# A one-core transformer layer: seven edits to where work stands in the order

## The chip, the core and the metric

The kernel runs on one core of one Trainium2 chip. A core has five engines, each with its own in-order instruction queue: PE (TensorE, the matrix engine; its weight loads are shown apart as PEld), DVE (VectorE), ACT (ScalarE), POOL (GpSimd) and SP (SyncE, which here only issues DMA transfers). They meet through semaphores. The metric is the device time of one execution in microseconds (us), and smaller is better.

## The reference, cut to what matters

One step of a streaming encoder layer. The two inputs are a prompt of 1024 frames and 64 frames of a running stream (1088 tokens in all), with a model width of 1024.

```python
mod = silu(c) @ w_ada + b_ada                                # shift1, scale1, gate1, shift2, scale2, gate2
h = rms_norm(x, g_norm1) * (1 + scale1) + shift1
c_q, c_kv, k_rope_raw, gq, gk, gv, g_lr, g_r = split(h @ w_in)
# group A: latent attention, 4 heads, chunk mask of 64 frames
latent = concat([past_latent, rms_norm(c_kv, g_kv_lora)])
kv = latent @ w_ukv                                          # per head: 128 key columns, 128 value columns
q = rms_norm(rms_norm(c_q) @ w_uq); k = rms_norm(concat([k_nope, krope]))   # then rotary, softmax, @ v
# group B: gated linear attention, 4 heads
log_a = log_sigmoid(g_lr @ w_gate_up + b_gate_up) / 16
b_out = rms_norm(gla_recurrence(gq, gk, gv, log_a, s0)) * silu(g_r)
x = x + gate1 * (concat([a_out, b_out]) @ w_out)
h2 = rms_norm(x, g_norm2) * (1 + scale2) + shift2
y = x + gate2 * (square(relu(h2 @ w_up)) @ w_down)           # MLP width 4096
```

The new latents, rotary keys and recurrent states are outputs too.

## The kernel before

All matrix products of the projections run three matmuls per block of 128 rows: operands are split into a rounded high part and the rest (`split`: an ACT copy makes the high part, a DVE subtraction the low part), and `mm3` (lines 93 to 95) multiplies high by high, high by low and low by high. So each operand costs an ACT and a DVE instruction before PE may use it, and most of PE's rows carry the lines 93, 94 and 95.

Tokens are in nine tiles (`TILES`: eight of 128 and one of 64, index 8, the running stream) or, for the first projections, three chunks (`CHUNKS`: 384, 384 and 320 tokens). PSUM has eight banks: four named `mm`, two named `tp` (transposes) and two named `g`.

What sets the order: each phase is a set of Python generators that yield (estimated PE time, wait, condition). `interleave` runs them against a made-up clock, always taking the first one that is ready, and the framework's own scheduler then places the instructions of each engine by its cost estimates, except those that `keep_in_program_order` pins. So a yield's number moves the place of what follows it only indirectly, and an edit in one generator moves others.

The stages that the change touches, in order of time:

- **First chunk** (`start`, `scales`, `normed`). While x, w_ada and the first columns of w_in are loaded, the sum of squares of chunk 0 is made: ACT squares eight blocks (line 325), DVE adds them 4+4, 2+2, 1+1 (line 330), PE sums over partitions (line 338), and the factor is spread by `dg` and a matmul with ones (line 357). PE makes the scale vector from w_ada (`scale_rows`, line 420), `scale_end` copies and transposes it (`lat`, lines 427 to 443). `split_first(hf, j)` makes `wh` and `wl` of half hf of column group j (lines 307 and 308). `normed` multiplies (line 378) and splits each block of x into `hh` and `hl`. Then `qk` runs group A0, A1 on the halves.
- **Gated linear attention** (`gla`). For each tile six or seven levels of `QL`,`KL` products (line 747), the output `o`, its norm `og` (line 802), and a `tail` that transposes og (line 808), scales it into `mog` and stores it. The tail of a tile runs within the next tile, at level 3.
- **Latents and gates** (`latents`, `gates`). `latents` runs the projection D1 (24 matmuls of 320 columns per tile), norms the 256 latent columns into `cn`, and one tile later transposes cn (line 644), scales it into `cl` (line 647, one buffer) and stores it in `lat_d`. At the same time `gates` takes, for each tile, g_r and the stored output of group B into two of four `gv` buffers (lines 825 and 826, both issued by SP), applies silu on ACT (line 829) and the product on DVE (line 830), and stores it (line 831).
- **Keys** (`keys_values`). Four tiles of past keys, then nine of new ones: 12 matmuls `g<-lath`, a norm over ACT, POOL and DVE (`kn`, line 907), then four transposes of kn (line 914) and four of the rotary part `krt` (line 921). The transposes stand behind a yield of 4500.
- **First MLP blocks** (`up`, `norm2`). The MLP runs a two-level product scheme with seven products per block. Product 1 of a block uses a `tp` bank. At the same time the last quarter of the second norm is under way: it spreads its factor into a `tp` bank (line 1387) that DVE reads in 16 instructions (line 1393).
- **Output** (`out`). The last product (4) of the down projection adds to 128 by 544 rows of y in two halves; the row block is stored once, after the second half.

Of the kernel before, what the change touches and what calls it, by code (L numbers as in the profile page):

```python
# [10 lines left out]
F32 = mybir.dt.float32  # L11
# [3 lines left out]
ALU = mybir.AluOpType  # L15
# [4 lines left out]
P = 128  # L20
# [11 lines left out]
HT = TOK // 2  # L32
# [39 lines left out]
def layer(ctx: ExitStack, tc: tile.TileContext, I, O):  # L72
# [12 lines left out]
    def tp_bank():  # L85
        return psT.tile([P, 512], F32, name="tp")
# [10 lines left out]
    def heads(ap):  # L97
        return ap.rearrange("p (h t) -> p h t", h=H)
# [176 lines left out]
    with ExitStack() as sctx:  # L275
# [43 lines left out]

        def scales(c):  # L320

# [6 lines left out]
            yield 600, 1000, None  # L328
            for n in (4, 2, 1):
                mm = DVE.tensor_tensor(out=sq[:, 0:n, :cn], in0=sq[:, 0:n, :cn],  # L330
                                                                   in1=sq[:, n:2 * n, :cn], op=ALU.add)
                if c == 0:
                    tc.keep_in_program_order(mm)
            yield 300, 1500 if c == 0 else 3000, None
            blocks = [(o, min(P, cn - o)) for o in range(0, cn, P)]
            pm = tp_bank()
            for j, (o, n) in enumerate(blocks):
                mm = PE.matmul(pm[:n, j:j + 1], lhsT=sq[:, 0, o:o + n], rhs=ones[:, 0:1], start=True, stop=True)
                if c == 0:
                    tc.keep_in_program_order(mm)  # L340
            st = xp.tile([P, 3], F32, name="st", bufs=2)
# [14 lines left out]
            for j, (o, n) in enumerate(blocks):  # L356
                mm = PE.matmul(bcs[c][:, o:o + n], lhsT=ones[:n, :], rhs=dg[:n, j, :n], start=True, stop=True)
                if c == 0:
                    tc.keep_in_program_order(mm)
            yield 600, 0, None  # L360

# [24 lines left out]
        def start():  # L386
            load_x(0)
            load_mod(0)
            load_first(0)
            load_mod(1)  # L390
            load_first(1)
            yield 0, 100, None
            load_x(1)
            acc = g_bank()
            for j in range(2):
                groups[GROUPS[j][0]] = [wp.tile([P, 8, 256], F32R, name=n) for n in ("wh", "wl")]
            a = scales(0)
            next(a)
            next(a)
            scale_rows(0, acc, range(4))  # L400
            next(a)
            scale_rows(0, acc, range(4, KT))
            for _ in a:
                pass
            split_first(0, 0)
            split_first(0, 1)
            scale_end(0, acc)
            yield 0, 0, has("mod 1 0")
            for n in "hl":
                h[n] = hpool.tile([P, KT, TOK + 2], F32R, name="h" + n)  # L410
            for c in range(3):
                if c:
                    yield 0, 4500, None
                    yield from scales(c)
                yield from normed(c)

# [118 lines left out]
    with gctx:  # L535
# [84 lines left out]
        def latents():  # L620
            yield 2000, 0, has("D1")
            for i in (8, 0, 1, 2, 3, 4, 5, 6, 7):
                off, n = TILES[i]
                s = i == 8
                ps = yield from rows("D1", off, n, 320)
                cn_ = dp.tile([P, 256], F32, name="cn")
                s2 = dp.tile([P, 2], F32, name="s2")
# [12 lines left out]
                while len(tails) > (0 if i == 7 else 1):  # L640
                    j, o2, n2, c2 = tails.pop(0)
                    tp = tp_bank()
                    for b in range(2):
                        PE.transpose(tp[:, b * P:b * P + n2], c2[:n2, b * P:(b + 1) * P], ident[:n2, :n2])
                    cl = dp.tile([P, 2, P], F32, name="cl", bufs=1)
                    for b in range(2):
# [8 lines left out]
        def gla():  # L655
# [56 lines left out]
            for i, (off, n) in enumerate(TILES):  # L712
# [23 lines left out]
                for lv, hf in enumerate(halves):  # L736
# [27 lines left out]
                    if lv == 2:  # L764
# [14 lines left out]
                        if i >= 7:  # L779
                            dst = O["st_s"] if smp else O["st_p"]  # L780
                            for p in range(2):
                                for j in range(2):
                                    SP.dma_start(dst[2 * p + j], sb_new[64 * j:64 * j + 64, p, P * j:P * j + P])
                    if lv == 3 and tail is not None:
                        tail()
                        tail = None
# [33 lines left out]
        def gates():  # L820

            yield 0, 2000, has("end C1", "gla out")
            for i, (off, n) in enumerate(TILES):
                r, mx = (gw.tile([P, 512], F32, name="gv", bufs=4) for _ in range(2))
                SP.dma_start(heads(r)[:, :, :n], r_d[:, :, off:off + n])
                SP.dma_start(heads(mx)[:, :, :n], mix_d[:, 4:8, off:off + n])
                yield 0, 1000, None
                r, mx = (heads(t)[:, :, :n] for t in (r, mx))
                ACT.activation(r, r, AF.Silu)
                (DVE if i % 2 else DVE).tensor_tensor(out=r, in0=r, in1=mx, op=ALU.mult)  # L830
                SP.dma_start(mix_d[:, 4:8, off:off + n], r)
# [44 lines left out]
    def keys_values(lh, ll, ki, tab, n, kv, slot):  # L876
# [33 lines left out]
        cs = slice(P * slot, P * slot + n)  # L910
        yield 0, 4500, None
        tp = heads(tp_bank())
# [506 lines left out]
    with ExitStack() as uctx:  # L1419
# [142 lines left out]
        def up():  # L1562
# [3 lines left out]
            def product(j, i, h):  # L1566
# [5 lines left out]
                elif i == 5:  # L1572
                    side[j, h] = g_bank()[:, 0:HT // 2]
                b = tp_bank()[:, 0:HT // 2] if i == 1 else side[j, h] if i > 4 else chain[j, h]
                for k in range(4):
# [101 lines left out]
    with ExitStack() as dctx:  # L1677
# [120 lines left out]
        def out(i, m, h, b):  # L1798
# [4 lines left out]
            for s, c0, c1 in SPANS:  # L1803
                c0, c1 = max(c0, h * HW), min(c1, h * HW + HW)
                if c0 < c1:
                    DVE.scalar_tensor_tensor(out=e[:, c0:c1], in0=b[:, c0 - h * HW:c1 - h * HW],  # L1806
                                             scalar=modT[:, 5, m0 + m, s:s + 1], in1=e[:, c0:c1], op0=ALU.mult, op1=ALU.add)
            if h and end:
                SP.dma_start(O["y_T"][(m0 + m) * P:(m0 + m + 1) * P, HT * th:HT * th + HT], e)

# [63 lines left out]
```

## Time and profile before

| | us |
|---|---|
| median of 3 runs | 1394.36 (1393.22 to 1397.86) |
| the profiled execution | 1394.88 |
| its span, first to last instruction | 1393.1 |
| PE busy in it | 1340.9 (96%) |
| PEld, DVE, ACT busy | 1261.0, 900.3, 685.3 |

A row of the timeline reads: start, duration, engine, line, operation, out<-in, partitions and elements, a count, and in brackets how long the engine sat idle before it and what it waited for. A row with a count stands for several instructions merged, and its duration is that of the group. Matmuls are pipelined: the step from one start to the next, not the duration, is what one costs. A row of the windows view reads: the stretch, its length, the busy time of each engine with its count of instructions, then the granted clock of PE as a share of full speed, the share of the DMA engines, and GB/s. A row of the waits view reads: who, for whom, total us, number of times, longest. A row of DMA issues gives the count, the size of each and the median time from issue to landing.

### The profile page before, as it was taken

The numbers are of one execution on the slowest core, as the hardware profiler recorded it, in microseconds if no ns is written. First come the engines' busy times: TensorE is split into PE (matmuls) and PEld (weight loads), VectorE is DVE, ScalarE is ACT, GpSimd is POOL, SyncE is SP. The second block draws the span as 40 slices with busy tenths as digits, with TensorE's granted clock in tenths as the row PEclk, the third lists the DMA queues.
The fourth block names the chain that finished last, engine by engine and source line by source line (L and its number), as shares of the span: only waits on it lengthen the run. The fifth ranks groups of instructions, "written<-read, shape, count | busy, mean of one in ns | idle before, by whom it ended". The sixth has DMA issues, their size and how long they took to land.

```text
span 1393.1 us, 26171 instructions
## 1 busy us (share of the span) xinstructions
PE 1340.9 (96%) x10014; PEld 1261.0 (91%) x10014; DVE 900.3 (65%) x2040; ACT 685.3 (49%) x1756; POOL 63.6 (5%) x115
## 2 busy tenths in 40 slices
PE   6998899988999999999999999999999999999998
PEld 5897789887876778899998999999999999999998
DVE  5688788337465766656789756566555866874554
ACT  5467667435345566653475544544444343343342
POOL 0010000011010210000000000000000000000000
PEclk9999999999999999999999999999999999999999
DMA  9320012384253442164225444444248764543440
GB/s 346 121 73 9 16 54 76 115 241 120 90 163 113 149 133 61 52 200 137 80 79 177 160 150 151 129 154 145 100 176 289 276 218 154 185 127 95 125 129 33
DMA packets 165591, 188.14 MB, mean 135 GB/s; under 512 B 16814, under 2 KB 116442, under 8 KB 165466
## 3 DMA queue, kind: packets, MB, share of 16 engines
q1 hardware_dynamic: 158010, 180.90, 40.5%
q10 hardware_dynamic: 7456, 5.57, 1.2%
q8 instruction: 79, 1.29, 0.4%
q14 instruction: 46, 0.38, 0.1%
HBM read 132.97 MB, written 53.46 MB: 134 GB/s over the span
## 4 chain that ended last, share of the span: by engine, by line
PE 82%; DVE 6%; ACT 4%; DMA 4%; issue 1%; POOL 1%; SPq 1%; DVEq 0%; ACTq 0%; POOLq 0%
PE mm L93 14%; PE mm L95 14%; PE mm L94 13%; PE g L93 6%; PE g L95 6%; PE g L94 6%; PE mm L992 3%; PE tp L93 3%; PE tp L95 3%; PE tp L94 3%; PE g L1019 3%; PE mm L166 2%; DMA raw<-in_w_in 1%; PE tp L1029 1%; PE g L747 1%
## 5 line engine op out<-in xcount | busy, mean ns | idle before, releaser
L101 ACT CAST opers<-quad 128x512 fp32r<-128x512 f32 x112 | 69.5, 620 | 184.5 <-PE mm L95 145.8
L102 DVE TENSOR_TENSOR opers<-quad,opers 128x512 fp32r<-128x512 f32 x112 | 77.2, 690 | 114.5 <-ACT opers L101 114.5
L95 PE MATMUL mm<-opers 128*128 128x272 f32 x448 | 128.9, 288 | 0.0
L93 PE MATMUL mm<-opers 128*128 128x272 f32 x448 | 128.5, 287 | 0.3 <-DVE e L1806 0.3
L94 PE MATMUL mm<-opers 128*128 128x272 f32 x448 | 128.3, 286 | 0.0
L93 PE MATMUL mm<-ah,wh 128*128 128x272 f32 x424 | 122.5, 290 | 3.4 <-ACT wh L101 2.2
L94 PE MATMUL mm<-al,wh 128*128 128x272 f32 x424 | 121.9, 288 | 0.0
L95 PE MATMUL mm<-ah,wl 128*128 128x272 f32 x424 | 121.8, 289 | 0.0
L93 PE MATMUL mm<-hh,wh 128*128 128x384 f32 (+2 forms) x264 | 90.7, 347 | 1.9 <-ACT hh L101 1.9
L95 PE MATMUL mm<-hh,wl 128*128 128x384 f32 (+2 forms) x264 | 87.5, 332 | 0.0
L94 PE MATMUL mm<-hl,wh 128*128 128x384 f32 (+2 forms) x264 | 87.4, 332 | 0.0
L93 PEld LDWEIGHTS mm<-opers 128*128 128x128 f32 x448 | 84.6, 189 | 0.5 <-issue 0.5
L95 PEld LDWEIGHTS mm<-opers 128*128 128x128 f32 x448 | 84.3, 188 | 0.0
L93 PEld LDWEIGHTS mm<-ah,wh 128*128 128x128 f32 x424 | 80.3, 189 | 4.2 <-ACT wh L101 2.6
L94 PEld LDWEIGHTS mm<-opers 128*128 128x128 f32 x448 | 84.0, 188 | 0.0
L94 PEld LDWEIGHTS mm<-al,wh 128*128 128x128 f32 x424 | 80.1, 189 | 0.0
L95 PEld LDWEIGHTS mm<-ah,wl 128*128 128x128 f32 x424 | 79.9, 189 | 0.0
L102 DVE TENSOR_TENSOR opers<-ru,opers 128x544 fp32r<-128x544 f32 x108 | 77.6, 719 | 2.2 <-ACT opers L101 2.0
L101 ACT CAST opers<-ru 128x544 fp32r<-128x544 f32 x108 | 69.4, 643 | 13.1 <-PE mm L95 11.7
L101 ACT CAST wh<-ru 128x512 fp32r<-128x512 f32 x67 | 41.3, 618 | 67.6 <-PE g L94 24.5
L102 DVE TENSOR_TENSOR wl<-ru,wh 128x512 fp32r<-128x512 f32 x67 | 45.9, 689 | 36.3 <-ACT wh L101 36.0
L93 PE MATMUL mm<-wh,hh 128*128 128x264 f32 (+3 forms) x216 | 66.4, 309 | 0.5 <-ACT gv L583 0.3
(409 smaller groups left out, 4310.4 us busy)
## 6 DMA issues: line engine op xcount, KB each, us to landing
ru<-u_d SPq DMA_DIRECT2D x108, 272.0 KB, 2.7
raw<-in_w_ada SPq DMA_DIRECT2D x40, 512.0 KB, 3.9
ru<-in_w_up SPq DMA_DIRECT2D x32, 512.0 KB, 4.1
quad<-in_w_down SPq DMA_DIRECT2D x16, 1024.0 KB, 6.6
u_d<-st SPq DMA_DIRECT2D x60, 272.0 KB, 2.1
u_d<-sc SPq DMA_DIRECT2D x45, 272.0 KB, 2.2
raw<-in_w_in SPq DMA_DIRECT2D x22, 256.0 KB, 4.2
x<-in_xo_T SPq DMA_DIRECT2D x8, 544.0 KB, 5.0
```

The costliest lines, as they stand in the source:

```text
L93: PE.matmul(out, lhsT=ah, rhs=bh, start=first, stop=False, skip_group_check=more)
L94: PE.matmul(out, lhsT=ah, rhs=bl, start=False, stop=False, skip_group_check=more)
L95: PE.matmul(out, lhsT=al, rhs=bh, start=False, stop=last, skip_group_check=more)
L101: ACT.copy(hi, src)
L102: eng.tensor_tensor(out=lo, in0=src, in1=f32(hi), op=ALU.subtract)
L166: mm = PE.matmul(acc[32 * j:32 * j + 32, 0:256], lhsT=scT[:, k, :], rhs=was[k][:, 256 * j:256 * (j + 1)], start=(k == 0), stop=(k == KT - ...
L747: PE.matmul(sc[:n, p, :, :n // 2], lhsT=kl[:, n * p:n * p + n], rhs=ql[:, :, p, :n // 2], start=True, stop=True)
L992: PE.matmul(sp[:n, :w], lhsT=x[:, hd, :n], rhs=y[:, hd, :w], start=(j == 0), stop=(j == 4))
L1019: PE.matmul(op[:n, 0:P], lhsT=pt[:kw, k, :n], rhs=kvs[kt // 4].v[:kw, kt % 4, hd], start=(kt == 0), stop=(kt == nkt - 1))
L1029: PE.transpose(tp[:kw, k, :n], pr[k0 // 4][:n, P * k:P * k + kw], ident[:n, :n])
```

## The change

- **First chunk by halves.** The squares of chunk 0 are added in two independent halves (0 to 3, 4 to 7), four DVE instructions in place of three; PE sums both (six matmuls of one column in place of three). `scale_end(0)` is called behind the first of the three spreading matmuls. `split_first(0, 0)` stays ahead of the normalisation, `split_first(0, 1)` goes behind its first two blocks.
- **Latents.** `cl` is gone: the transposed latents are written into the place of the `cn` they came from, and cn has three buffers in place of two.
- **Tail of gated linear attention** at level 5 in place of 3.
- **Gates.** The loads of tile i+1 are issued before tile i is computed; the yield ahead of silu is 2500 in place of 1000. There are still four gv buffers.
- **Keys.** The yield ahead of the kn transposes is 6500 in place of 4500.
- **First MLP blocks.** Product 1 of blocks 0 and 1 uses a `g` bank in place of a `tp` bank.
- **Output.** For the last product each half of 272 columns is stored as soon as it is added, eight stores in place of four.

```diff
-            for n in (4, 2, 1):
-                mm = DVE.tensor_tensor(out=sq[:, 0:n, :cn], in0=sq[:, 0:n, :cn],
-                                                                   in1=sq[:, n:2 * n, :cn], op=ALU.add)
+            for a, n in ((0, 2), (0, 1), (4, 2), (4, 1)) if c == 0 else ((0, 4), (0, 2), (0, 1)):
+                mm = DVE.tensor_tensor(out=sq[:, a:a + n, :cn], in0=sq[:, a:a + n, :cn],
+                                       in1=sq[:, a + n:a + 2 * n, :cn], op=ALU.add)
...
+            halves = (0, 4) if c == 0 else (0,)
             for j, (o, n) in enumerate(blocks):
-                mm = PE.matmul(pm[:n, j:j + 1], lhsT=sq[:, 0, o:o + n], rhs=ones[:, 0:1], start=True, stop=True)
+                for k in halves:
+                    mm = PE.matmul(pm[:n, j:j + 1], lhsT=sq[:, k, o:o + n], rhs=ones[:, 0:1], start=(k == 0),
+                                   stop=(k == halves[-1]))
...
+                    if j == 0:
+                        between()
...
-            a = scales(0)
+            a = scales(0, lambda: scale_end(0, acc))
...
+            split_first(0, 0)
             for _ in a:
                 pass
-            split_first(0, 0)
-            split_first(0, 1)
-            scale_end(0, acc)
...
-                yield from normed(c)
+                steps = normed(c)
+                if c == 0:
+                    for _ in range(4):
+                        yield next(steps)
+                    split_first(0, 1)
+                yield from steps
...
-                cn_ = dp.tile([P, 256], F32, name="cn")
+                cn_ = dp.tile([P, 256], F32, name="cn", bufs=3)
...
-                    cl = dp.tile([P, 2, P], F32, name="cl", bufs=1)
+                    cl = c2.rearrange("p (b t) -> p b t", b=2)
...
-                    if lv == 3 and tail is not None:
+                    if lv == 5 and tail is not None:
...
+            def load(i):
+                off, n = TILES[i]
                 r, mx = (gw.tile([P, 512], F32, name="gv", bufs=4) for _ in range(2))
                 SP.dma_start(heads(r)[:, :, :n], r_d[:, :, off:off + n])
                 SP.dma_start(heads(mx)[:, :, :n], mix_d[:, 4:8, off:off + n])
-                yield 0, 1000, None
...
+            load(0)
+            for i, (off, n) in enumerate(TILES):
+                if i + 1 < len(TILES):
+                    load(i + 1)
+                yield 0, 2500, None
...
-        yield 0, 4500, None
+        yield 0, 6500, None
...
-                b = tp_bank()[:, 0:HT // 2] if i == 1 else side[j, h] if i > 4 else chain[j, h]
+                b = ((g_bank if j < 2 else tp_bank)()[:, 0:HT // 2] if i == 1 else side[j, h] if i > 4 else
+                     chain[j, h])
...
-            if h and end:
-                SP.dma_start(O["y_T"][(m0 + m) * P:(m0 + m + 1) * P, HT * th:HT * th + HT], e)
+            rows = O["y_T"][(m0 + m) * P:(m0 + m + 1) * P, HT * th:HT * th + HT]
+            if i == 4:
+                SP.dma_start(rows[:, h * HW:h * HW + HW], e[:, h * HW:h * HW + HW])
+            elif h and end:
+                SP.dma_start(rows, e)
```

The scheduler decides what the edits do to each queue. At three places the prediction rests on it. ACT's queue in the first chunk, from the squares of chunk 0 on; `wh` is the split of the first columns of w_in, `lat` the copy of the scale vector, `hh` the high part of a block of x. Before:

```order
L325 ACTIVATE sq<-hf 128x1536 x2
L307 CAST wh<-raw 128x512 x4
L427 COPY lat<-g 128x128
L101 CAST hh<-hf 128x384 x3
L427 COPY lat<-g 128x128
L307 CAST wh<-raw 128x512 x2
L101 CAST hh<-hf 128x384
L307 CAST wh<-raw 128x512 x2
```

The change:

```order
L325 ACTIVATE sq<-hf 128x1536 x2
L307 CAST wh<-raw 128x512 x2
L435 COPY lat<-g 128x128
L101 CAST hh<-hf 128x384 x2
L307 CAST wh<-raw 128x512 x2
L101 CAST hh<-hf 128x384 x2
L435 COPY lat<-g 128x128
L307 CAST wh<-raw 128x512 x4
```

Two of the four copies of wh are now behind the scale vector and two blocks of x, and the fourth block comes ahead of the copies of the second half. DVE's queue where chunk 1 begins (`st` and `dg` are the factor of chunk 1, `hf` its first blocks, `sq` of 4x320 the squares of chunk 2). Before:

```order
L348 TENSOR_SCALAR st<-tp 128x3
L353 TENSOR_SCALAR dg<-ident,st 128x128 x3
L330 TENSOR_TENSOR sq<-sq 128x4x320
L378 SCALAR_TENSOR_TENSOR hf<-hf,G_89,g 128x384 x3
L102 TENSOR_TENSOR hl<-hf,hh 128x384 x3
```

The change:

```order
L351 TENSOR_SCALAR st<-tp 128x3
L356 TENSOR_SCALAR dg<-ident,st 128x128 x3
L383 SCALAR_TENSOR_TENSOR hf<-hf,G_89,g 128x384 x3
L102 TENSOR_TENSOR hl<-hf,hh 128x384 x3
L383 SCALAR_TENSOR_TENSOR hf<-hf,G_89,g 128x384 x3
L102 TENSOR_TENSOR hl<-hf,hh 128x384 x3
L383 SCALAR_TENSOR_TENSOR hf<-hf,G_89,g 128x384 x2
L330 TENSOR_TENSOR sq<-sq 128x4x320
```

The first addition of the squares of chunk 2 has moved from ahead of chunk 1's blocks to behind the eighth. ACT's queue in D1, where `cn` and `kraw` belong to one tile of latents, `gv` is the silu of a tile of gates, and `cl` (in the change: `cn<-tp`) the transposed latents. Before:

```order
L829 ACTIVATE gv<-gv 128x512
L632 COPY kraw<-mm 128x64
L637 DMA out_lat_p<-lat 128x256
L829 ACTIVATE gv<-gv 128x512
L647 ACTIVATE cl<-tp,vT 128x128 x2
L628 ACTIVATE cn,s_3473<-mm 128x256
L632 COPY kraw<-mm 128x64
```

The change, at the corresponding place:

```order
L847 ACTIVATE gv<-gv 128x512
L645 DMA out_lat_p<-lat 128x256
L847 ACTIVATE gv<-gv 128x512
L636 ACTIVATE cn,s_3380<-mm 128x256
L656 ACTIVATE cn<-tp,vT 128x128 x2
L640 COPY kraw<-mm 128x64
L645 DMA out_lat_p<-lat 128x256
L847 ACTIVATE gv<-gv 128x512
L636 ACTIVATE cn,s_3429<-mm 128x256
```

A tile's scaled latents now stand directly behind the next tile's cn, one silu to a tile; at one place two silus stand one behind the other, as before.

More of the change, by code (lines that the diff above doesn't have):

```diff
@@ L318, in first_groups, with scales @@
                 yield 0, 700, None
-        def scales(c):
+        def scales(c, between=None):
             c0, cn = CHUNKS[c]
@@ L336, in scales @@
             pm = tp_bank()
+            halves = (0, 4) if c == 0 else (0,)
             for j, (o, n) in enumerate(blocks):
-                mm = PE.matmul(pm[:n, j:j + 1], lhsT=sq[:, 0, o:o + n], rhs=ones[:, 0:1], start=True, stop=True)
-                if c == 0:
-                    tc.keep_in_program_order(mm)
+                for k in halves:
+                    mm = PE.matmul(pm[:n, j:j + 1], lhsT=sq[:, k, o:o + n], rhs=ones[:, 0:1], start=(k == 0),
+                                   stop=(k == halves[-1]))
+                    if c == 0:
+                        tc.keep_in_program_order(mm)
             st = xp.tile([P, 3], F32, name="st", bufs=2)
@@ L414, in start @@
                     yield from scales(c)
-                yield from normed(c)
+                steps = normed(c)
+                if c == 0:
+                    for _ in range(4):
+                        yield next(steps)
+                    split_first(0, 1)
+                yield from steps
         def scale_rows(hf, acc, ks):
@@ L822, in gates @@
             yield 0, 2000, has("end C1", "gla out")
-            for i, (off, n) in enumerate(TILES):
+            tiles = {}
+            def load(i):
+                off, n = TILES[i]
                 r, mx = (gw.tile([P, 512], F32, name="gv", bufs=4) for _ in range(2))
@@ L826, in gates @@
                 SP.dma_start(heads(mx)[:, :, :n], mix_d[:, 4:8, off:off + n])
-                yield 0, 1000, None
-                r, mx = (heads(t)[:, :, :n] for t in (r, mx))
+                tiles[i] = [heads(t)[:, :, :n] for t in (r, mx)]
+            load(0)
[3 more added lines that the diff above has]
+                yield 0, 2500, None
+                r, mx = tiles.pop(i)
                 ACT.activation(r, r, AF.Silu)
-                (DVE if i % 2 else DVE).tensor_tensor(out=r, in0=r, in1=mx, op=ALU.mult)
+                DVE.tensor_tensor(out=r, in0=r, in1=mx, op=ALU.mult)
                 SP.dma_start(mix_d[:, 4:8, off:off + n], r)
```

## The prediction

> **What bounds the kernel now.** I read the page's busy times and chain first, then the waits of PE.
>
> ```profile
> span 1393.1 us, 26171 instructions
> ...
> PE 1340.9 (96%) x10014; PEld 1261.0 (91%) x10014; DVE 900.3 (65%) x2040; ACT 685.3 (49%) x1756; POOL 63.6 (5%) x115
> ...
> PE 82%; DVE 6%; ACT 4%; DMA 4%; issue 1%; POOL 1%; SPq 1%; DVEq 0%; ACTq 0%; POOLq 0%
> ```
>
> PE is busy for 1340.9 of 1393.1 us and carries 82% of the chain. The change takes no product away, so it can only win from the 52 us in which PE is not busy, and from stretches in which PE is busy but slow. The waits of PE say who holds it up:
>
> ```profile
> PE g L420 <- DMA ada<-in_w_ada: 8.1, 5, 6.5
> PE tp L914 <- DVE kn L907: 6.9, 6, 1.7
> PE tp L644 <- ACT cl L647: 4.5, 2, 3.7
> ...
> PE tp L93 <- DVE x L1393: 1.9, 1, 1.9
> ...
> PE tp L808 <- DVE og L802: 1.8, 2, 1.0
> ```
>
> Four of these five are places that the change edits: keys 6.9, latents 4.5, the first MLP blocks 1.9, the tails 1.8. The first belongs to w_ada's arrival, whose order of loads is not changed. The windows view shows the second kind of loss, the granted clock (the value after POOL):
>
> ```profile
> 295.90:301.20 5.30, 1.59 (x12) 1.33 (x11) 1.54 (x3) 1.61 (x6) 0.78 (x2) 1.00 0.88 245
> 301.20:304.60 3.40, 3.40 (x15) 3.40 (x14) 0.91 (x2) 0.84 (x2) 0.43 (x1) 0.51 1.00 269
> ...
> 720.50:724.40 3.90, 1.96 (x16) 1.77 (x15) 3.90 (x11) 3.58 (x12) 0.00 (x0) 1.00 0.02 4
> 724.50:727.90 3.40, 3.40 (x17) 3.40 (x17) 2.73 (x8) 3.30 (x11) 0.00 (x0) 0.50 0.01 2
> 728.00:753.00 25.00, 22.34 (x169) 21.26 (x169) 24.66 (x54) 14.68 (x33) 0.00 (x0) 1.00 0.35 103
> ```
>
> Right behind the stall in the latents and the one in the MLP, PE runs 3.4 us at half clock. A stall there costs more than its own length.
>
> **The change part by part.** All terms are against the profiled execution, 1394.88 us.
>
> *Latents and gates.* The 3.71 us stall, read from ACT and PE:
>
> ```profile
> 298.74 0.63 ACT L829 ACTIVATE gv<-gv 128x512 f32<-128x512 f32 x1 [2.74 <-DMA gv<-r_d]
> 299.27 0.61 ACT L647 ACTIVATE cl<-tp,vT 128x128 f32<-128x128 f32 x2
> ...
> 299.93 0.44 PE L644 MATMUL tp<-ident,cn 128*128 128x128 f32 x2 [3.71 <-ACT cl L647]
> ...
> 302.02 0.47 PE L95 MATMUL mm<-wh,hl 128*128 128x320 f32 x1
> 302.29 0.47 PE L93 MATMUL mm<-wh,hh 128*128 128x320 f32 x1
> ...
> 309.11 0.31 PE L93 MATMUL mm<-wh,hh 128*128 128x320 f32 x1
> 309.26 0.31 PE L94 MATMUL mm<-wl,hh 128*128 128x320 f32 x1
> ```
>
> PE waits for cl, but cl stands behind a silu that waited 2.74 us for its g_r. Both edits bear on it: the load goes a tile ahead, and the ACT order puts cl directly behind the next tile's cn. What stays is that tile i+2 needs the buffers of tile i, so its load waits for the landing of tile i's product. By the order, silus 4 and 5 stand back to back, and a loop of silu 0.63, product 0.69, store, and two landings falls between them. A tile of D1 takes 24 steps of 0.148 = 3.55 us (309.11 to 309.26); silu 5 comes some 2 us late for it, of which PE sees about 1 us, since cn is needed only one tile later. So of the 4.5 us I take 3.5 (bounds 1.5, if two such waits come, and 4.5). The half clock: steps of 0.27 (302.02 to 302.29) in place of 0.148, for 12 matmuls, is 1.4 us; it goes with the stall (bounds 0 and 1.5). Together **-4.9**.
>
> The Trainium skill, "TensorE: Matmul & The Clock Gate", Part 1, says that PE's clock drops to half after at least one idle window of about 3.4 us, and that the windows run free of the program. The latents' stall agrees; the MLP's does not, since there the row of 720.50 shows PE busy for half of the 3.9 us ahead of the slow stretch. The trace decides: about 2 us of idleness in a window is enough here. By the rule, the MLP stall's removal would leave that slow stretch where it is.
>
> *First chunk.*
>
> ```profile
> 13.01 1.41 PE L338 MATMUL tp<-ones,sq 128*128 128x1 f32 x6 [1.19 <-DVE sq L330]
> ...
> 16.28 2.49 DVE L308 TENSOR_TENSOR wl<-raw,wh 128x512 fp32r<-128x512 f32 x4
> 19.29 1.66 DVE L378 SCALAR_TENSOR_TENSOR hf<-hf,G,g 128x384 f32<-128x384 f32 x3
> ...
> 26.01 0.44 PE L93 MATMUL mm<-hh,wh 128*128 128x384 f32 x1 [0.88 <-ACT hh L101]
> ...
> 39.96 1.49 DVE L330 TENSOR_TENSOR sq<-sq 128x1280 f32<-128x1280 f32 x1 [0.71 <-ACT sq L325]
> ...
> 42.85 0.44 PE L93 MATMUL mm<-hh,wh 128*128 128x384 f32 x1 [0.98 <-ACT hh L101]
> ```
>
> Adding by halves lets the sums start about 1.2 us sooner, the wait in the first row, but there are twice as many, 1.41 us more: nothing won, about +0.2. Moving two of the four wl behind the scale vector takes half of 2.49 off DVE ahead of it; PE's transpose of the vector is then the limit, and the first block starts about 0.95 us earlier than 19.29. The two wl come back behind the second block, ahead of nothing that PE needs yet. The wait at 26.01 (a block behind two copies of wh) goes, as the ACT order shows. For chunk 1, DVE did 0.71 of waiting and 1.49 of adding for chunk 2 ahead of its first block; that is behind the eighth block now, so the 0.98 of PE at 42.85 mostly goes. The parts overlap: the largest sum is 0.95 + 0.88 + 0.98 = 2.8, the least is 0.5, since the second half of w_in lands at a time that the change does not move. I take **-1.5**.
>
> *Keys.*
>
> ```profile
> 317.85 0.40 PE L95 MATMUL g<-wh,latl 128*128 128x512 f32 x1
> 321.99 0.66 PE L914 MATMUL tp<-ident,kn 128*128 128x128 f32 x4 [0.95 <-DVE kn L907]
> ...
> 338.90 0.40 PE L95 MATMUL g<-wh,latl 128*128 128x512 f32 x1
> 344.13 0.63 PE L914 MATMUL tp<-ident,kn 128*128 128x128 f32 x4 [1.67 <-DVE kn L907]
> ...
> 426.36 0.63 PE L914 MATMUL tp<-ident,kn 128*128 128x128 f32 x4 [0.89 <-DVE kn L907]
> ...
> 500.44 0.63 PE L914 MATMUL tp<-ident,kn 128*128 128x128 f32 x4 [0.77 <-DVE kn L907]
> ```
>
> From the last matmul to kn takes 4.1 to 5.2 us (317.85 to 321.99, 338.90 to 344.13). In the changed order the transposes of the last eight keys stand behind 5.3 us or more of PE's other work, so the waits at 426.36 and 500.44 go: **-1.6** (bounds 0 and 1.7). For the four past tiles and the first new one the scheduler has hardly moved them: 24, 17, 16, 17 and 15 matmuls of projection lie between, where 19, 16, 18 and 13 with 12 before. At 0.148 to 0.18 each that is 2.5 to 3.5 us, still short of 4.1 to 5.2. Their waits, 6.9 - 1.7 = 5.2 in the view, stay or grow a little: **+0.5** (bounds -1.0 and +2.5).
>
> *Tails.*
>
> ```profile
> 161.93 0.66 PE L808 MATMUL tp<-ident,og 128*128 128x128 f32 x4 [1.02 <-DVE og L802]
> ...
> 215.23 0.66 PE L808 MATMUL tp<-ident,og 128*128 128x128 f32 x4 [0.78 <-DVE og L802]
> ```
>
> In the changed order the first of these has kept its place, behind the same eight matmuls; the second has seven more ahead of it, over 1 us. So **-0.8** (bounds -1.8, and +1.0 if mog's four ACT instructions delay the next tile's QL, for which PE waited up to 1.2 us).
>
> *First MLP blocks.*
>
> ```profile
> 722.99 0.36 PE L93 MATMUL tp<-ah,wh 128*128 128x272 f32 x1 [1.94 <-DVE x L1393]
> ...
> 747.21 0.39 PE L93 MATMUL mm<-ah,wh 128*128 128x272 f32 x1 [1.41 <-ACT wh L101]
> ```
>
> With a g bank PE need not wait for DVE's 16 reads. But DVE is busy for 24.66 of the 25 us from 728 (the last windows row), splitting the tokens and weights that PE needs next, and at 747.21 PE waits for it. PE comes there 1.94 us earlier, or 3.6 with the slow stretch's 1.7 (half of 3.4), and waits that much longer. DVE's own work is the same and in nearly the same order. **-0.3** (bounds 0 and -3.6).
>
> *Output.*
>
> ```profile
> 1389.53 0.62 DVE L1806 SCALAR_TENSOR_TENSOR e<-mm,modT,e 128x240 f32<-128x240 f32 x2 [0.25 <-PE mm L95]
> ...
> ru<-u_d SPq DMA_DIRECT2D x108, 272.0 KB, 2.7
> ...
> quad<-in_w_down SPq DMA_DIRECT2D x16, 1024.0 KB, 6.6
> ```
>
> Behind the last addition only the last store is left; it shrinks from 272 to 136 KB. Between the two sizes quoted 752 KB cost 3.9 us, so 136 KB cost 0.7; a store's fixed part may be larger. **-0.5** (bounds 0 and -1.0).
>
> The sum: -4.9 - 1.5 - 1.6 + 0.5 - 0.8 - 0.3 - 0.5 = -9.1, so 1385.8 for the profiled execution. That lies 0.5 above the median of the three runs, so I forecast **1385.3**. With all terms at their good ends the sum is -18, at their bad ends it is +1.5.
>
> **The rivals.**
>
> *The MLP edit pays in full.* If DVE, freed of the bank, gets ahead too, 3.6 goes in place of 0.3: 1382.0. For it: the stall and its slow stretch are in plain sight. Against: DVE's full window.
>
> *The latents still wait.* Four gv buffers hold two tiles, so every load still waits for a store's landing, and a silu still stops ACT ahead of a cl. Then the 4.9 does not come: 1390.2. For it: the two silus back to back, and SP issuing all of this in one queue with the stores of latents and keys. Against: the measured wait was for a load issued just before it was needed.
>
> *Later keys starve the attention* (slower). The last eight keys' transposes stand behind 6.2 us of work on average, 4.0 before, so each tile's keys are ready some 2.2 us later. Attention of a tile starts only with its keys. If PE has no other unit, eight tiles pay up to 17.5 us, 1402.8; from 1.14 us a tile (9.1 / 8) on, the change loses. Against it:
>
> ```profile
> 480.00:620.00 140.00, 137.60 (x997) 122.51 (x996) 89.99 (x244) 86.70 (x230) 9.75 (x14) 1.00 0.36 107
> ```
>
> PE lacks 2.4 us in 140 here: other units fill in.
>
> **How the numbers follow.** The forecast gets 0.58, the full MLP gain 0.13, the waiting latents 0.21, the starved attention 0.08. A measurement of this kernel tells about 0.3% (4.2 us) from no change, so faster means below 1390.2. The forecast lies there nearly always (0.96), the first rival always, the second in 0.4 of cases, the third hardly: 0.78 faster, 0.16 the same, 0.06 slower. The range 1380.5 to 1391.0 holds the forecast with most of its bounds and the first two rivals; it leaves out the third and the far ends.
>
> **What would show it.** Right: no stall above 1.5 us and no half clock in D1; kn waits near 5 us in total, all before 400; the wait at the MLP's first blocks gone and a longer one about 25 us behind it; chunk 1's first matmul about 1.5 us earlier. Wrong: silu waits that still end in PE's, kn waits gone in the past tiles, PE waiting for keys between 400 and 620, or half clocks at new places.

## The result

The changed kernel takes 1397.24 us (median of 20 runs, 1394.97 to 1399.55) where the kernel before, run beside it, takes 1394.78 (20 runs, 1392.66 to 1399.23). The ratio is 1.0015, with a 95% interval of 1.0008 to 1.0021: slower by about 2 us. The forecast was 9 us faster, and the time lies outside the range given. The page of the changed kernel's profiled execution (1396.91 us):

```profile
span 1395.1 us, 26185 instructions
...
PE 1347.8 (97%) x10020; PEld 1262.8 (91%) x10020; DVE 900.6 (65%) x2041; ACT 685.1 (49%) x1756; POOL 64.6 (5%) x115
```

PE is idle for 5 us less than before (1395.1 - 1347.8 = 47.3 against 52.2), the way that was forecast, but busy for 6.9 us more with six matmuls more. So the loss is first of all busy time: PE is slower at nearly the same work. The granted clock over the whole span is 0.991 in both executions, so it is not more half clock in total. The waits of PE:

```profile
PE tp L652 <- DVE cn L638: 4.0, 3, 3.2
PE tp L1047 <- ACT prob L1021: 3.8, 3, 2.5
PE tp L932 <- DVE kn L925: 3.7, 5, 1.1
...
PE mm L93 <- ACT wh L101: 2.2, 2, 1.8
...
PE tp L1151 <- ACT mo L1062: 2.0, 1, 2.0
```

The latents' wait is still there, now named after `cn`. The keys' waits have shrunk from 6.9 to 3.7, and one for `mo`, which before did not have, has come.

Where the time went is read best from when the same matmul starts in the two timelines. Stage by stage, each from its first matmul to the next one's, in us:

| stage | before | change | change without the later keys | later keys alone | gates by pairs |
|---|---|---|---|---|---|
| to the first QL,KL product | 103.4 | 100.3 | 100.2 | 103.7 | 101.8 |
| gated linear attention, to D1 | 175.8 | 174.0 | 173.4 | 176.8 | 173.8 |
| D1 and past keys, to the first kh,qh | 125.0 | 120.9 | 122.1 | 122.5 | 115.7 |
| attention, to the first mh,wh | 196.0 | 205.1 | 197.8 | 204.9 | 196.5 |
| output, to the first ah,wh | 106.2 | 107.6 | 106.2 | 107.6 | 106.1 |
| MLP, to the last matmul | 682.9 | 683.4 | 682.5 | 682.6 | 682.6 |

(The last three columns are runs of the next section.) Where the attention begins, the change is 8.9 us ahead; the terms of the forecast up to there (latents, first chunk, tails, past keys) come to 6.7. Part of the 8.9 is luck: in the gated linear attention the granted clock was 0.98 in this execution and 0.96 in the one of before, by an estimate from these two shares some 3.5 us (0.02 x 175). Executions with the same edits up to there differ as much (0.95 in the change with w_out's splits later, below). In the attention the change loses 9.1. The 1.5 us of the output stage are the attention's too: by the windows view PE does 855 matmuls there in place of 843, since that many more of the attention's stand behind the first mh,wh. The windows view of the attention, before and after:

```profile
404.14:600.13 195.99, 191.51 (x1345) 154.28 (x1343) 131.17 (x387) 119.81 (x373) 20.85 (x30) 0.99 0.36 109
```

```profile
395.20:600.33 205.13, 198.51 (x1343) 155.31 (x1342) 133.08 (x389) 119.71 (x372) 23.38 (x32) 0.98 0.36 110
```

Practically the same matmuls, 7.0 us more busy time and 2.1 more idle. Most of the idle time lies in a few microseconds at the end. The changed kernel's timeline there, ACT and then PE:

```profile
581.39 1.04 ACT L1181 CAST wh<-raw 128x1024 fp32r<-128x1024 f32 x1 [2.13 <-DMA raw<-in_w_out]
582.35 0.36 ACT L1062 ACTIVATE mo<-g,sta 128x128 f32<-128x128 f32 x1
583.55 1.04 ACT L1181 CAST wh<-raw 128x1024 fp32r<-128x1024 f32 x1 [0.84 <-DMA raw<-in_w_out]
584.50 0.36 ACT L1062 ACTIVATE mo<-g,sta 128x128 f32<-128x128 f32 x1
...
587.01 0.78 ACT L1021 ACTIVATE prob<-mm,sta,ssq 128x512 f32<-128x512 f32 x1 [0.91 <-DVE sta L1017]
```

```profile
584.91 0.55 PE L1151 MATMUL tp<-ident,mo 128*128 128x128 f32 x3 [2.00 <-ACT mo L1062]
587.93 1.11 PE L1047 MATMUL tp<-ident,prob 128*128 128x128 f32 x4 [2.47 <-ACT prob L1021]
```

ACT stands 2.13 and 0.84 us for weights of w_out, which belong to the next stage, with `mo` and the last exponentials (`prob`) of the attention queued behind; the exponentials then wait another 0.91 us for DVE. PE stands for those. Before, only three of the six splits stood ahead of the last eight exponentials. And the clock, in windows of 3.4 us (after POOL: the granted clock):

```profile
582.10:585.50 3.40, 1.36 (x11) 0.89 (x9) 2.70 (x3) 2.56 (x5) 0.00 (x0) 1.00 0.71 187
585.54:592.36 6.82, 4.43 (x15) 3.74 (x16) 2.94 (x12) 5.80 (x14) 0.00 (x0) 0.50 0.72 209
735.70:739.10 3.40, 1.12 (x7) 0.68 (x5) 3.40 (x10) 2.18 (x6) 0.00 (x0) 1.00 0.34 99
739.14:745.96 6.82, 6.34 (x27) 6.28 (x28) 6.82 (x20) 2.34 (x4) 0.00 (x0) 0.50 0.20 69
```

The stall is followed by 6.8 us at half clock; so is another one at the MLP's first blocks (the last two rows).

### The profile page after: what moved, and what is told of

It is laid out like the page before. It is cut to its first block, busy times and chain, and to the rows that moved or that the text cites. A ratio compares the mean times of both kernels' runs of the same rounds, so it can differ in the third digit from the quotient of the medians.

```text
span 1395.1 us, 26185 instructions
## 1 busy us (share of the span) xinstructions
PE 1347.8 (97%) x10020; PEld 1262.8 (91%) x10020; DVE 900.6 (65%) x2041; ACT 685.1 (49%) x1756; POOL 64.6 (5%) x115
## 4 chain that ended last, share of the span: by engine, by line
PE 80%; DVE 7%; ACT 5%; DMA 4%; issue 2%; POOL 1%; SPq 0%; DVEq 0%; ACTq 0%; POOLq 0%
PE mm L93 14%; PE mm L94 13%; PE mm L95 13%; PE g L93 6%; PE g L95 6%; PE g L94 5%; PE mm L1010 3%; PE tp L93 3%; PE tp L94 3%; PE tp L95 3%; PE g L1037 2%; PE mm L166 2%; PE g L756 1%; PE tp L1047 1%; DMA mix_d<-gv 1%
```

## The experiments

Each run was timed against the kernel before on the same chip, whose median moved between 1394.2 and 1395.7, so differences are read from the ratios. The profiled runs also differ by one to three slow stretches of 3.4 us (each costs at most 1.7 us, half of its length) at places that an edit did not touch; a difference of 2 us in one trace is therefore no evidence by itself.

**Which edit costs the time.** In the planned orders of kernels with one edit each, only the keys' number moves the splits of w_out on ACT (L1181) against the last exponentials of the attention, and the traces of the edits run alone below agree. So first it alone, then all but it. (The output's edit was not run alone.)

```diff
-        yield 0, 4500, None
+        yield 0, 6500, None
         tp = heads(tp_bank())
         for hd in range(H):
             PE.transpose(tp[:, hd, :n], kn[:n, hd], ident[:n, :n])
```

> The kernel before with one edit, the key transposes' yield 6500 in place of 4500. Theory A (the later keys cost the time): in the order of this kernel all six splits of w_out's first columns stand ahead of the last eight exponentials of the attention on ACT, as in the changed kernel, where before three of them stood behind two; so PE stands idle and at half clock near the attention's end, and the time is 1399 to 1403, 5 to 8 us above before. Theory B (my prediction's term, the loss came from another edit): 1392 to 1394, 1 us below before, with kn waits near 5 in place of 6.9 us.

Measured: 1402.48 us, ratio 1.0056 (1.0039 to 1.0072). Its waits:

```profile
PE tp L914 <- DVE kn L907: 4.5, 4, 1.7
PE tp L1029 <- ACT prob L1003: 3.8, 3, 2.5
PE tp L1133 <- ACT mo L1044: 2.4, 1, 2.4
```

The kn waits fall by 2.4 us, as the edit was to bring about; the new wait for mo and the longer one for prob are those of the change.

> The changed kernel with the key transposes' yield back at 4500. Theory A: the end of the attention is as before and the other edits keep what they won up to there (4.9 us at the first latents by the two traces), so 1388 to 1391. Theory B: the later keys won 1 us, so without them 1398.

Measured: 1387.20 us, ratio 0.9944 (0.9927 to 0.9962). Theory A holds on both sides. One number costs 7 to 8 us by itself and, by the two ratios, 10 us in the change (1.0015 against 0.9944); the six other edits win 8 us. The columns of the change and of the change without the later keys show that it is the attention that differs, 205.1 against 197.8 us.

**Is it the splits of w_out on ACT?** The later keys kept, but w_out's splits later too:

```diff
-        yield from wo_loader(range(5), lambda: [wp.tile([P, 20, P], F32R, name=n) for n in ("wh", "wl")])
+        yield from wo_loader(range(5), lambda: [wp.tile([P, 20, P], F32R, name=n) for n in ("wh", "wl")], wait=10000)
```

> The changed kernel, later keys included, with one number more altered: w_out's first split waits 10000 in place of 4000 in the planner, so on ACT the six splits stand ahead of the last 6, 6, 6, 6, 4 and 2 exponentials in place of 8. Theory A1 (the splits, waiting for w_out's arrival ahead of the last softmax, make the stalls of 2.0 and 2.5 us and the slow stretch behind them): 1391 to 1394 against 1397.2, with the waits for mo and for the last prob gone. Theory A2 (the last tile's attention has no other work beside it whatever ACT does, since its keys are late): 1396.5 to 1398.5, the waits stay.

Measured: 1394.74 us, ratio 0.9991 (0.9978 to 1.0003). By the ratios (1.0015 to 0.9991) 3.3 us are won back, at the low end of what A1 expected (3.2 to 6.2 below 1397.2). In the trace the wait for mo and the slow stretch are gone and the attention takes 201.2 us. The waits for prob stay, against A1: 4.1 us in total where the change has 3.8, the longest of them:

```profile
597.64 0.66 PE L1047 MATMUL tp<-ident,prob 128*128 128x128 f32 x4 [2.03 <-ACT prob L1021]
```

So the splits ahead of the softmax are a part, some 4 of the 9 us in the traces of this stage (205.1 to 201.2), and not all of it.

A2, that too little other work is left for PE at the end, is not settled by this run, and the traces show something of its kind. Measured from the first matmul of the attention, the last keys are transposed at 98.0 us without the later keys (493.72 - 395.69) and at 116.7 with them (511.93 - 395.20); before the change it was 96.3. That is 18.7 us later, near the eight times 2.2 us that the prediction's rival reckoned with. The rows, first without the later keys, then of the change:

```profile
493.72 0.63 PE L932 MATMUL tp<-ident,kn 128*128 128x128 f32 x4 [0.78 <-DVE kn L925]
```

```profile
511.93 0.63 PE L932 MATMUL tp<-ident,kn 128*128 128x128 f32 x4
```

The query projection, which runs beside the attention, is not later. Its last matmul stands 168.0 us behind the attention's first one before (404.14), and 166.5 us in the change (395.20):

```profile
572.17 0.34 PE L95 MATMUL g<-wh,cql 128*128 128x384 f32 x1
```

```profile
561.74 0.34 PE L95 MATMUL g<-wh,cql 128*128 128x384 f32 x1
```

So 38.6 us of the stage are left behind it where 28.0 were (to 600.33 and to 600.13). What this costs was not measured by itself.

**Past keys or new keys?**

```diff
-        yield 0, 4500, None
+        yield 0, 6500 if ki >= 8 else 4500, None
```

> The change with the 6500 for the four past tiles alone and 4500 for all new ones. In the order the attention's end is as in the kernel before. Theory A: 1386.5 to 1388, the same as with 4500 everywhere (1387.2), since the cost sits in the new keys. If the past tiles carry part of the cost or a gain of their own: 2 us or more away from 1387.2.

Measured: 1387.83 us, ratio 0.9943 (0.9928 to 0.9959), the same as with 4500 everywhere. The cost sits in the new keys, in the attention. The later transposes bring nothing for the past tiles that a measurement could tell.

**What else slows PE in the attention.** One group in the view by lines stands out, the products of the modulation (w_ada), in the same two stages, of before and of the change:

```profile
L166 PE MATMUL mm<-raw,scT 128*32 128x256 f32 x222 | 22.1, 392 | 0.0
```

```profile
L166 PE MATMUL mm<-raw,scT 128*32 128x256 f32 x224 | 25.6, 391 | 0.0
```

3.5 us more for the same products. The timeline of the change shows how: parted groups (x2 and x6) take as long as whole ones (x8).

```profile
406.36 0.62 PE L166 MATMUL mm<-raw,scT 128*32 128x256 f32 x2
406.91 0.52 PE L1047 MATMUL tp<-ident,prob 64*128 64x64 f32 x5
...
407.76 0.63 PE L166 MATMUL mm<-raw,scT 128*32 128x256 f32 x6
408.33 0.45 PE L1010 MATMUL mm<-kh,qh 128*64 128x512 f32 x1
...
412.18 0.64 PE L166 MATMUL mm<-raw,scT 128*32 128x256 f32 x8
412.75 0.24 PE L1010 MATMUL mm<-khs,qh 128*64 128x64 f32 x1
```

From start to next start: 0.55 us for two, 0.57 for six, 0.57 for eight. The order of the change has 51 groups, the one of before 44. To see whether that is the rest of the price, the products were pinned to the program's order, which parts fewer of them:

```diff
-                if not ahead:
-                    tc.keep_in_program_order(mm)
+                tc.keep_in_program_order(mm)
```

> The changed kernel with w_out's splits later (1394.7) and the modulation products (line 166) pinned to the order of the program, so that the four of one block of w_ada are seldom parted: 42 groups in place of 51 on PE. By the trace a group costs 0.55 us whether it has two matmuls or eight. Theory C1 (the rest of the later keys' price is those parted groups): 9 x 0.55 = 5 us less, 1389 to 1391. Theory C2 (a parted group only takes time that PE would have waited anyway): 1393.5 to 1396.

> The kernel with the gates by pairs and without the later keys (1382.8), with the modulation products pinned in the same way: 39 groups in place of 44. Theory C1: 5 x 0.55 = 2.8 us less, 1379 to 1381. Theory C2: 1382 to 1384.

Measured: 1404.78 us, ratio 1.0081 (1.0065 to 1.0098), and 1387.88 us, ratio 0.9957 (0.9945 to 0.9970; the kernel that it was made from is the gates by pairs, below, 0.9907). Both slower, but the pin also caught the first modulation in the first chunk: the second kernel's first QL,KL product starts at 107.2 us, where it was 101.8 without the pin. So these two answered nothing about the attention, and the pin was set there alone:

```diff
-                if not ahead:
+                if not ahead or pin:
                     tc.keep_in_program_order(mm)
...
-            yield from mod_vec(m, rawp, "raw", aw, mm_bank, 3)
+            yield from mod_vec(m, rawp, "raw", aw, mm_bank, 3, pin=True)
```

> The changed kernel with w_out's splits later (1394.7) and the modulation products pinned in the attention alone, not in the first chunk, where the pin of the run before cost 5 us by 52 us: 43 groups in place of 51. Theory C1 (parted groups are the rest of the later keys' price): 8 x 0.55 = 4.4 us less, 1389.5 to 1391.5. Theory C2, by the trace of the run before (the products took 5.6 us less, and PE's waits and pieces elsewhere 12 us more from 374 us to the attention's end): 1398 to 1403, slower, since a pin also holds the product behind whatever stands ahead of it in the program.

> The gates by pairs without the later keys (1382.8), the same pin in the attention alone: 40 groups in place of 44. Theory C1: 4 x 0.55 = 2.2 us less, 1380 to 1381.5. Theory C2: 1382 to 1384, what the products win being lost to waits, as between 366 and 592 us of the run before (226.5 against 226.1 us).

Measured: 1398.82 us, ratio 1.0027 (1.0016 to 1.0037; without the pin 0.9991), and 1385.00, ratio 0.9928 (0.9916 to 0.9940; without it 0.9907). C1's forecast fails. In the first of the two the products take 19.9 us where they took 25.6, and the stage is longer all the same, 202.5 against 201.2; its waits for prob grew from 4.1 to 5.6:

```profile
PE tp L1047 <- ACT prob L1021: 5.6, 5, 2.0
PE tp L1047 <- DVE kl L934: 1.2, 1, 1.2
```

Taking these products together in this way turns most of their time into waits. Whether parted groups cost anything on the whole stays open, and with it a half to two thirds of the later keys' price (moving the splits won back 3.9 of 7.3 us in the traces of the attention, and 3.3 of 10 by the ratios): the runs show that it comes with the new keys' order, not through which instruction. The longer end of the attention, shown above, is a candidate that no run tests.

**The latents and gates alone.** The edits as in the change: three cn, cl in cn's place, the gate loads a tile ahead.

> The kernel before with the edits of latents and gates alone (three cn, cl in cn's place, the gate loads a tile ahead). The prediction's term: the stall of 3.7 us and its slow stretch go, 1389 to 1391. Rival, by the trace of the changed kernel, where PE still waits 3.2 us for a cn behind a silu that waits for its load: 1393.5 to 1395, the same within 1 us.

Measured: 1392.55 us, ratio 0.9981 (0.9968 to 0.9993). About half of the forecast, and not where it was to come from:

```profile
PE tp L644 <- DVE cn L630: 5.5, 4, 3.4
PE tp L924 <- DVE kn L917: 4.5, 5, 1.2
```

The latents' waits are no shorter than before (5.5 with one of 3.4, against 4.5 with one of 3.7); the keys' have fallen from 6.9 to 4.5, all of it ahead of the attention (5.3 to 2.8), though this run does not edit the keys. Why the stall stays is seen in the change's own trace, D1 around it, ACT, then POOL, DVE and PE:

```profile
295.01 0.63 ACT L847 ACTIVATE gv<-gv 128x512 f32<-128x512 f32 x1 [2.46 <-DMA gv<-r_d]
295.55 0.36 ACT L636 ACTIVATE cn<-mm 128x256 f32<-128x256 f32 x1
...
296.94 0.48 DVE L638 TENSOR_SCALAR cn<-mm,s 128x256 f32<-128x256 f32 x1 [3.46 <-POOL s L121]
...
297.48 0.44 PE L652 MATMUL tp<-ident,cn 128*128 128x128 f32 x2 [3.24 <-DVE cn L638]
```

A silu still waits 2.46 us for its g_r, though its load stands a tile ahead in the program; now the norm of the next tile stands behind it on ACT, and POOL's s, DVE's cn and PE's transpose behind that. The load was not issued a tile ahead. It is the sixth load of g_r, for the sixth silu, on SP's queue before and in the change:

```profile
293.89 0.82 SPq L825 DMA_DIRECT2D gv<-r_d  x1
```

```profile
290.57 0.53 SPq L837 DMA_DIRECT2D gv<-r_d  x1
```

Before, the silu starts 4.85 us behind the issue (298.74), in the change 4.44 (295.01). Three runs ask why the load is late.

> The change without its later keys (1387.2), and six buffers for the gates in place of four, loads two tiles ahead. Theory B1 (the silus wait because a buffer's load must wait for the store of two tiles before): the silus' waits and PE's 3.7 us for cn go, 1382.5 to 1384.5. Theory B2 (the transfers themselves are at their limit there, the DMA engines being 95% busy from 284 to 299): the waits stay above 2 us, 1386 to 1388.5.

```diff
-                r, mx = (gw.tile([P, 512], F32, name="gv", bufs=4) for _ in range(2))
+                r, mx = ((gw.tile([P, 512], F32, name="gx", tag="ST") if i % 3 == 2 else
+                          gw.tile([P, 512], F32, name="gv", bufs=4)) for _ in range(2))
...
             load(0)
+            load(1)
...
-                if i + 1 < len(TILES):
-                    load(i + 1)
+                if i + 2 < len(TILES):
+                    load(i + 2)
```

Measured: 1388.24 us, ratio 0.9939 (0.9922 to 0.9955), the same as with four (0.9944). PE still waits, 2.78 us at 302.65, and the DMA engines are full (the last value but one):

```profile
280.00:290.00 10.00, 8.69 (x60) 8.34 (x59) 5.34 (x9) 4.65 (x16) 1.92 (x6) 1.00 1.02 285
290.00:300.00 10.00, 9.88 (x69) 9.59 (x67) 3.72 (x7) 2.68 (x9) 1.29 (x3) 1.00 0.92 258
```

This fits B2, but it does not settle it. The median from issue to landing of these loads is 4.7 us in place of the change's 4.0. But SP, which issues in the order of its queue, still waits in this run for a store of the gates to land before it issues a load (line 839), and what stands behind that load in the queue waits too:

```profile
SPq L839 <- DMA mix_d<-gv: 1.4, 1, 1.4
```

Full DMA engines and a queue held up behind stores are therefore not told apart. Then the gates left out altogether (no loads, silu, product or store, so that half of the output is missing):

> The change without its later keys, and the gates left out (no loads of g_r, no silu, no product and no store, so the gated half of the output is missing). It prices the gates beside D1. If the loads and silus of the gates cause the stall of 3.7 us and the slow stretch: 1381 to 1384. If D1's own stores and norm cause it: 1386 to 1388.

Measured: 1381.65 us, ratio 0.9894 (0.9876 to 0.9912). So the gates cost 7 us by the ratios (0.9944 to 0.9894), and the stall is theirs: from 290 to 300 us PE is busy for 9.73 of 10 us, at a DMA share of 0.24.

```profile
290.00:300.00 10.00, 9.73 (x60) 8.86 (x60) 3.43 (x9) 3.08 (x16) 0.88 (x3) 1.00 0.24 73
```

Last, the gates kept but cut otherwise, a pair of heads by 256 tokens:

```diff
+            pieces = [(g, k) for g in range(2) for k in range(5)]
...
+            def at(t, g, k):
+                o, w = 256 * k, min(256, TOK - 256 * k)
+                return t[:, 4 * (t is mix_d) + 2 * g:4 * (t is mix_d) + 2 * g + 2, o:o + w], w
...
-                SP.dma_start(heads(r)[:, :, :n], r_d[:, :, off:off + n])
-                SP.dma_start(heads(mx)[:, :, :n], mix_d[:, 4:8, off:off + n])
+                for src in (r_d, mix_d):
+                    t = gw.tile([P, 512], F32, name="gv", bufs=4).rearrange("p (h t) -> p h t", h=2)
+                    a, w = at(src, g, k)
+                    SP.dma_start(t[:, :, :w], a)
```

> The change without its later keys, with the gates cut otherwise: a pair of heads by 256 tokens in place of four heads by 128, so each run of bytes in their transfers is 1 KB in place of 512 bytes, and the pieces of the first pair no longer depend on the second pair's columns; in the order five of the ten silus stand ahead of D1's first norm, where two of nine did. Still four buffers. If what holds D1 up is that the gates' transfers fill the DMA engines there: PE's waits for cn under 2 us, 1382.5 to 1385.5. If the same bytes cost the same however they are cut and whenever they start: 1386.5 to 1388.5.

Measured: 1382.77 us, ratio 0.9907 (0.9894 to 0.9921), 13 us below the kernel before and the fastest that computes everything. The windows from the end of the gated linear attention to past D1, without later keys: first with the gates as in the change, then by pairs.

```profile
245.00:272.00 27.00, 27.00 (x164) 23.47 (x163) 8.55 (x24) 8.16 (x28) 1.19 (x2) 1.00 0.35 111
272.00:300.00 28.00, 23.51 (x152) 22.20 (x151) 9.69 (x16) 11.38 (x33) 4.10 (x10) 0.96 0.89 239
```

```profile
245.00:272.00 27.00, 27.00 (x162) 23.16 (x161) 12.24 (x29) 15.26 (x44) 2.39 (x4) 1.00 0.66 201
272.00:300.00 28.00, 28.00 (x193) 27.30 (x191) 12.70 (x30) 13.47 (x43) 4.87 (x12) 1.00 0.77 226
```

Half of the gates' work moves into a stretch where the DMA engines were 0.35 busy, because the first pair's pieces need only the first group's columns; in D1 PE no longer stands at all (28.00 of 28). The run changed two things at once, the size of a piece and when it may start, and does not tell them apart.

**The MLP's bank, the first chunk and the tail, each alone,** as in the change's diff.

> The kernel before with one edit, product 1 of the first two MLP blocks in a g bank. Theory of the prediction (DVE bounds the stretch behind it): the wait of 1.9 us and the slow stretch move some 15 us on, and the time is 1394.1 to 1395.2, within 0.5 of before. Rival (it pays in full): 1391, 3.6 below before.

Measured: 1394.21 us, ratio 0.9995 (0.9983 to 1.0007). The wait at the first blocks is gone, and this one stands 13 us behind it:

```profile
735.73 0.43 PE L93 MATMUL mm<-ah,wh 128*128 128x272 f32 x1 [1.76 <-ACT wh L101]
```

The full gain of 3.6 us lies outside the interval (0.0017 of 1395 is 2.4 us).

> The kernel before with the edits of the first chunk alone. The prediction's term is 1.5 us: 1393.0 to 1394.0, and 2.1 us by the trace of the changed kernel at 48 us (45.84 against 47.91): 1392.5 to 1393.5. Rival (what is won there is lost again in the gated linear attention, whose waits and slow windows fall differently): 1394.5 to 1396.

Measured: 1391.89 us, ratio 0.9977 (0.9966 to 0.9988): 1.7 to 4.7 us won. By its trace the first block of `hh,wh` starts at 19.30 against 21.09 us and the first QL,KL product at 101.89 against 103.41, so 1.5 to 1.8 of it can be followed in the trace; the rival is out.

> The kernel before with the tail of the gated linear attention at level 5 alone. The prediction's term is 0.8 us: 1393.5 to 1394.6. Rival, by the trace of the changed kernel (the second wait for og, 0.8, is gone and a wait of 1.0 for QL stands 3 us behind it): 1394.8 to 1395.8, nothing won.

Measured: 1394.65 us, ratio 0.9994 (0.9985 to 1.0003). Neither 0.8 us nor nothing is excluded. In its trace the second wait for og is gone, and where it stood PE waits for QL, which before it did not:

```profile
213.59 0.68 PE L747 MATMUL g<-QL,KL 128*128 128x128 f32 x4 [1.03 <-DVE QL L695]
```

## Why the prediction was wrong

**The step that failed is the cost of the later keys.** It was priced by the kn waits alone: -1.6 for the new tiles, +0.5 for the past ones. The waits did what the term said and a little more: 4.5 in place of 6.9 us in the run with this edit alone, with none left behind 404 us. But that run is 0.56% slower, and the change without the edit 0.56% faster than before. The rival "later keys starve the attention" had the right sign and place, and a chance of 0.08; what the prediction set against it, that PE lacks only 2.4 us in 140, was taken to mean that other units would always fill in. This overlap is what the prediction had wrong. It holds until the last tiles, while the keys fall 18.7 us behind (116.7 against 98.0), and then the projection that filled in is done (its last matmul at 166.5 of the stage's 205.1 us). From 446 to 580 us the changed kernel's PE is as busy as ever:

```profile
446.00:580.00 134.00, 133.03 (x916) 109.13 (x909) 85.16 (x250) 80.79 (x245) 14.72 (x20) 1.00 0.30 92
```

The loss does not come at every tile, as the rival had it, but as stalls at the end, a slow stretch behind them, and slower products on the way, whose share in the time stays open. The number moved not only the transposes: with it all six splits of w_out, which wait for their weights, stand ahead of the last eight exponentials on ACT. Moving the splits away won back 3.3 us; for the rest, a half to two thirds of the price, the cause is open. The orders that the prediction read were those around the keys; the stalls came at 582 to 588 us, behind the last keys, and no row of the trace of before shows them.

**Latents and gates: -4.9 forecast, about -2.6 measured alone (0.9968 to 0.9993, so 1.0 to 4.5), by another way.** The stall stayed at 3.2 us, with its slow stretch. That is the second rival, which had 0.21. Whether its reasons were right is open: six buffers in place of the four do not help, but SP's queue, which it also named, was not freed by them. What the prediction did not weigh stood in a row that it quoted, the DMA share of 0.88 and 1.00 in D1, and it took an earlier place in the program for an earlier issue.

**First chunk: -1.5 forecast, 1.7 to 4.7 measured**; the term was right or a little small. **MLP bank: -0.3 forecast,** nothing told from zero, with the stall moved on as described, though by 13 us and not by 25; right, and the first rival is out. **Tails: -0.8,** not told from zero by its time; in the trace of that edit alone the wait of 0.8 only changed into one of 1.0 for QL, the way that the term's bad end described, though the row names DVE and not ACT's copies to mog. **Output: -0.5 forecast;** from the last matmul's start to the end of the span it is 3.8 us against 3.9, so 0.1 by two traces; not run alone.

The slow stretches in D1, at the attention's end and in the MLP do follow stalls, as the prediction read them; with the MLP bank alone the one of 724.5 moved along with the stall, to 736 us. But the forecast counted only those that would go. The two new ones, at 585 and 739 us, are each twice as long as the one there was in the MLP before. Two of the prediction's own signs of being wrong came: a silu's wait that still ends in PE's, and half clock at new places.

## What to carry to other kernels

An edit of one number in a planned order must be followed to the end of the phase, on every engine: look above all at what of the next phase is placed ahead of the last work of this one, what it waits for, and how much other work is left to fill in there. Before loading earlier or adding buffers, read when the load is really issued, and the DMA share of the stretch. Here, at shares around 0.9, an earlier place in the program and two more buffers did not end the stall; cutting the transfers otherwise, with half of them in a stretch where the engines were free, was worth 5 us more (0.9944 to 0.9907). And with several edits in one change, run all but one: the one that loses can hide a gain four times the change's own difference.

## What was not expected of the hardware

Half clock does not need a window without work. In the window of 3.4 us ahead of the slow stretch PE was busy for 1.36 us, 40%, in the attention, and for 1.12 at the MLP's blocks, and both times 6.8 us at half clock followed. The Trainium skill, "TensorE: Matmul & The Clock Gate", Part 1, asks for an idle window of about 3.4 us; these rows differ, and they decide. Nor are the 2 us of idleness, which the prediction took to be enough, a threshold: with the later keys alone PE was busy for 1.65 of 3.40 us in one window, and full clock followed. And the latents' stall before, which the prediction took to agree with that Part, had PE busy for 1.32 us in the 3.4 us ahead of its slow stretch. The rows, first with the later keys alone, then before:

```profile
728.80:732.20 3.40, 1.65 (x14) 1.43 (x12) 3.12 (x10) 3.08 (x10) 0.00 (x0) 1.00 0.00 0
732.24:735.65 3.41, 3.27 (x25) 3.18 (x25) 2.81 (x7) 3.41 (x12) 0.00 (x0) 1.00 0.02 7
```

```profile
297.84:301.25 3.41, 1.32 (x10) 1.32 (x10) 1.38 (x2) 1.51 (x5) 0.83 (x2) 1.00 0.81 222
```

Products on 32 columns of PE (line 166): a group of two takes 0.55 us, a group of eight 0.57. In the program each block of w_ada is four products, one to each quarter of PE's columns, and the trace shows two records for a product (320 for 160), so that one alone takes as long as four together.
